# A diffusion layer's fill stage: second up column's weight sums made beside the mixing stage, last tiles' gated sums kept in accumulators, first token sums split ahead of the prompt's norm

## Chip, cores and metric

One core of a Trainium2 chip. Its engines run side by side, each in its own order: TensorE (PE) for matmuls, VectorE (DVE), ScalarE (ACT) and GpSimd (POOL) for elementwise work; SP's queue, and POOL's, issue DMA transfers. The metric is the device time of one execution in microseconds (us), the median of several runs. Profiles are of one execution each.

## What is computed

One layer over 1024 sample tokens and 128 prompt tokens of width 1024, all in 32-bit floats: a gated linear-attention mixer, then a convolutional feed-forward net, both with a residual. The edits lie where the one ends and the other begins:

```python
mix = merged @ w_out
x = x + gate1 * mix
h = rmsnorm(x, norm2) * (1 + scale2) + shift2
u = dw_conv(h @ w_up, conv_w, conv_b, grid)
gate, up = jnp.split(u, 2, axis=-1)
x = x + gate2 * ((silu(gate) * up) @ w_down)
```

FFN_HIDDEN is 2816, so `w_up` is 1024 x 5632. modulation (gate1, scale2, shift2) differs between sample and prompt.

## The kernel before

**Stages.** Up to about 730 us the mixer runs. Then the products with w_out for nine tiles of 128 tokens (0 to 7 sample, 8 prompt) with residual, norm and modulation, to about 790. Then 22 columns of 128 hidden units of the up-projection (L1724, L1925) with the convolution on DVE (L1862, L1879), to about 1284, and the products with w_down to the end.

**Splits.** Each 32-bit operand is a rounded high part (`hi`, made by ACT) and the rest (`lo`, by a subtraction in `split_lo`, L69), and a product is three matmuls: hi x hi, hi x lo, lo x hi.

**Up products.** A column's weights are 2 x 2 blocks ("11" to "22": row 1 the gate, row 2 the up half; 512 inputs each). With four sums of weights (s1 to s4) and four of token blocks (t1 to t4), seven products with names `up(c, 1)` to `up(c, 7)` replace eight block products. So each column needs eight weight blocks, hi and lo, and the tokens once need b11, b21, b22, t1, t2, t3 and t4, hi and lo. `half_hi` and `half_lo` split half a token block, `token_sum` makes a sum; `rb(i, j, n)` is a half of a raw token block, `tmp` are sums in the accumulator tiles `acc`. `up_prompt` are the same column's products with the prompt (tile `p`, parts ph and pl).

**Column 0's weights** are made beside the end of the mixer by `prepare_up()`: four loads into two tiles named up (one pair of blocks each), eight high parts (`up_hi`), eight low parts (four in tiles `up_lo`, four in place), four sums (L1294), and sixteen stores by POOL to scratch memory (scr_up, L1291). `up_hi` and `up_lo` come from the pool `fb`, which has two buffers (`fbp = pool(es1, "fb", 2)`). Their memory is used again by later pools of the w_out stage. SP later loads the parts from scratch into the weight slots W and W0 (`load_first`, L1746). **Later columns** get raw weights by `load_row`, sums by `weight_sums` (L1715 to L1718; column 1's on DVE, the rest on POOL), high parts by ACT (L1709) and low parts by POOL (`split_slots`, tiles wuh and wul).

**Tiles of tokens.** For a tile t: `head7(t)` or `heads(t, a, b)` are its products with w_out into an accumulator us[t] (pool of three in PSUM); `mult` (L1407) multiplies by the gate into xn, `add` (L1410) adds the residual xt and stores it, `square` (L1415, ACT) and `stat` (POOL's power, L1420) give the norm, `norm` (L1423, ACT) applies it. PE then transposes: `turn3(g, kt)` (L1431) for tiles 0 to 2 and 3 to 5 (groups 0 and 1), `turn2` (L1452) for 6 and 7, `turn_prompt` (L1468) for 8; `modulate3`, `modulate2` and `modulate_prompt` write the raw token blocks, half on DVE (L1364) and half on ACT (L1360). `load_mh(t)` and `load_xt(t)` are SP's loads of mixer output and residual for a tile.

**What sets the order.** Most instructions around the change go through `run(engine, ...)`, which ties each to the one before it on its engine, so engines run in the order in which the code is written; DMA issues follow their position and waits, and a buffer that is used again makes the next writer wait for the last reader. `ran["free"] = True` lifts the tie.

Of the kernel before, what the change touches and what calls it, by code (L numbers as in the profile page):

```python
# [13 lines left out]
ALU = mybir.AluOpType  # L14
# [35 lines left out]
def kernel(ctx: ExitStack, tc: tile.TileContext, ins, outs, stop=None):  # L50
# [46 lines left out]
    scr_up = [dram.tile([P, 8, 512], F32, name=f"scr_up{x}") for x in "hl"]  # L97
# [1173 lines left out]
    def prepare_up():  # L1271

        r = {}
        for row in (1, 2):
            t = rawp.tile([P, 2, 512], F32, name="up0", tag="raw")
            for half in range(2):
                nm = f"{row}{half + 1}"
                r[nm] = t[:, half]
                c0 = (row - 1) * HID
# [5 lines left out]
        def split(nm, place, keep):  # L1285
# [4 lines left out]
            for i, t in enumerate((hi, lo)):  # L1290
                nc.gpsimd.dma_start(scr_up[i][:, UP0.index(nm)], t.bitcast(F32))  # L1291
# [17 lines left out]
    prepare_up()  # L1309
# [37 lines left out]
    x4q = pool(es2, "x4", 1)  # L1347
    mhq = pool(es2, "mh", 1)
# [36 lines left out]
    us, xts, xns, sts, mhs_, turned = {}, {}, {}, {}, {}, {}  # L1385
# [18 lines left out]
    def mult(t):  # L1404
        q = {"n3": xaq, "n4": x4q}.get(X_OUT[t], xnq)
        xns[t] = q.tile([P, D], F32, name="xn2", tag=X_OUT[t])
        run("dve", lambda: tt(xns[t], us[t], gate1[0 if t == 8 else 1], op=ALU.mult))  # L1407

    def add(t):
        run("dve", lambda: tt(xts[t], xns[t], xts[t], op=ALU.add))  # L1410
        nc.gpsimd.dma_start(scr_x1[t], xts[t])

    def square(t):
        sts[t] = accs[0][:, 1024 + 2 * t : 1026 + 2 * t]
        run("act", lambda: nc.scalar.activation(xns[t], xts[t], AF.Square, accum_out=sts[t][:, 0:1]))  # L1415
# [6 lines left out]
    def norm(t):  # L1422
        run("act", lambda: nc.scalar.activation(xns[t], xts[t], AF.Copy, scale=sts[t][:, 1:2]))  # L1423
# [49 lines left out]
    def modulate_prompt(kt):  # L1473
        scaled(kt, 0, again["p"][:, kt, :], turned["p", kt // 4][:, kt % 4, :])
# [69 lines left out]
    for kt in range(0, KT, 2):  # L1544
# [26 lines left out]
    for kt in range(0, KT, 2):  # L1571
# [5 lines left out]
        if kt == 0:  # L1577
# [3 lines left out]
        if kt == 2:  # L1581
            stat(6)
            norm(6)
            load_xt(8)
    heads(7, 6, 8)
    token_sum(tmp[0], rb(0, 1, 0), rb(0, 0, 0))
    half_hi("b11", 1, rb(0, 0, 1))
    token_sum(tmp[2], rb(1, 1, 0), tmp[0])
    half_hi("b21", 1, rb(1, 0, 1))
    half_lo("b11", 1, rb(0, 0, 1))  # L1590
    half_lo("b21", 1, rb(1, 0, 1))
    mult(7)
    add(7)
    square(7)
    stat(7)
    norm(7)

    heads(8, 0, 5)
    wot = again["wo"]
    for nm in ("b22", "t2"):  # L1600
        for x in "hl":
            HB[x][nm] = wot.tile([P, 4, 512], F32R, name=f"{nm}{x}", tag="wo")
    half_hi("b22", 0, rb(1, 1, 0))
    half_lo("b22", 0, rb(1, 1, 0))
    turn2(0)
    turn2(1)
    heads(8, 5, 6)
    turn2(2)
# [666 lines left out]
```

## Time and profile before

| | us |
|---|---|
| median of 3 runs | 1565.24 (1563.28 to 1569.36) |
| profiled execution: its time | 1569.81 |
| profiled execution: its span | 1568.0 |
| PE busy | 1496.2 (95%) |
| DVE busy | 1148.0 (73%) |
| ACT busy | 782.1 (50%) |
| POOL busy | 706.0 (45%) |
| mean granted PE clock, of full | 0.985 |

The span runs from the first to the last instruction; the time also holds what lies around it, 1.8 us. Rows of a timeline begin with start and duration, and end with the idle time before them and what ended it. A window's row gives for each engine its busy time and, in brackets, its instructions, then PE's granted clock (1.00 is full), the share of the 16 DMA engines, and GB/s.

### The profile page before, as it was taken

What the parts mean: (1) busy time and instruction counts of PE and PEld (TensorE: products, weight loads), DVE (VectorE), ACT (ScalarE), POOL (GpSimd) and SP (SyncE); (2) the same over time, 40 slices, a digit from 0 to 9 for tenths busy, and PEclk for the clock granted to TensorE, in tenths of its full rate; (3) what the DMA queues carried; (4) which work ended last, traced back from release to release, by engine and by line L of the source; (5) the groups of instructions that cost most, each with busy time, mean ns of one, the idle gap of its engine ahead of it and who ended that gap; (6) DMA issues with size and microseconds to landing.
All of it is one profiled execution on the core that took longest, in us unless ns stands there. A gap on an engine that the chain in (4) does not pass through costs nothing.

```text
span 1568.0 us, 31139 instructions
## 1 busy us (share of the span) xinstructions
PE 1496.2 (95%) x12506; PEld 1260.1 (80%) x12506; DVE 1148.0 (73%) x1735; ACT 782.1 (50%) x1519; POOL 706.0 (45%) x538
## 2 busy tenths in 40 slices
PE   7999999999999989899888999999999998999997
PEld 2699989999898978677666888888888887788886
DVE  3657566565566667555569999999999999579565
ACT  3565567545454445513554444544444444457444
POOL 1512122334332240132126899999999996000001
PEclk9999999999999999999999999999999999999999
DMA  9311111336445452777541455455645566879763
GB/s 341 104 55 46 46 53 60 113 99 197 123 136 166 127 171 86 281 281 251 180 151 56 166 167 135 123 139 135 190 117 146 163 162 209 311 239 355 251 191 118
DMA packets 172939, 252.49 MB, mean 161 GB/s; under 512 B 11732, under 2 KB 113602, under 8 KB 170874
## 3 DMA queue, kind: packets, MB, share of 16 engines
q1 hardware_dynamic: 149591, 172.21, 34.4%
q0 software_dynamic: 22592, 77.60, 15.9%
q8 instruction: 98, 1.61, 0.4%
q10 hardware_dynamic: 611, 0.68, 0.1%
q14 instruction: 47, 0.39, 0.1%
HBM read 190.62 MB, written 82.90 MB: 174 GB/s over the span
## 4 chain that ended last, share of the span: by engine, by line
PE 72%; DVE 9%; DMA 6%; issue 4%; ACT 4%; POOL 3%; SPq 1%; POOLq 0%; ACTq 0%; DVEq 0%
PE u L1724 23%; PE mm L603 13%; PE xb L2137 6%; PE yb L2137 6%; PE mm L617 5%; PE x L1925 3%; DVE acc L1862 3%; PE mm L746 3%; PE lv L935 3%; PE yb L2188 2%; PE x L1003 1%; PE mm L506 1%; DMA raw<-in_w_in_dram 1%; DMA mh<-scr_m 1%; DMA wa<-in_w_ada_dram 1%
## 5 line engine op out<-in xcount | busy, mean ns | idle before, releaser
L1862 DVE SCALAR_TENSOR_TENSOR acc<-u,convc,acc 128x945 f32<-128x945 f32 (+2 forms) x352 | 426.8, 1218 | 8.4 <-ACT acc L1850 1.3
L69 POOL TENSOR_TENSOR wl<-raw,wh 128x1024 fp32r<-128x1024 f32 x42 | 103.5, 2467 | 241.4 <-ACT wh L132 182.7
L603 PE MATMUL mm<-h1h,wh 128*128 128x384 f32 x528 | 186.0, 352 | 1.1 <-ACT qj L515 1.1
L603 PE MATMUL mm<-h1l,wh 128*128 128x384 f32 x528 | 180.1, 341 | 0.0
L603 PE MATMUL mm<-h1h,wl 128*128 128x384 f32 x528 | 180.0, 341 | 0.0
L898 DVE TENSOR_TENSOR Q<-Q,fb 128x384 f32<-128x384 f32 x126 | 81.1, 644 | 90.9 <-PE lv L935 89.5
L69 POOL TENSOR_TENSOR wul<-sr,wuh 128x512 fp32r<-128x512 f32 (+1 forms) x65 | 118.2, 1819 | 28.2 <-ACT wuh L1709 28.0
L69 POOL TENSOR_TENSOR wul<-ra,wuh 128x1024 fp32r<-128x1024 f32 x44 | 111.6, 2536 | 20.0 <-ACT wuh L1709 17.5
L888 ACT ACTIVATE m<-k 128x384 f32<-128x384 f32 x126 | 70.3, 558 | 85.3 <-PE lv L935 40.1
L2112 POOL TENSOR_TENSOR sq<-sq,mhalf 128x1 f32<-128x1 f32 x9 | 11.0, 1229 | 215.5 <-DVE sq L2109 215.5
L603 PEld LDWEIGHTS mm<-h1h,wh 128*128 128x128 f32 x528 | 100.3, 190 | 6.0 <-issue 3.9
L603 PEld LDWEIGHTS mm<-h1l,wh 128*128 128x128 f32 x528 | 100.4, 190 | 0.6 <-issue 0.2
L603 PEld LDWEIGHTS mm<-h1h,wl 128*128 128x128 f32 x528 | 100.0, 189 | 0.8 <-issue 0.5
L617 PE MATMUL mm<-wh,h1h 128*128 128x256 f32 x288 | 83.7, 291 | 1.6 <-ACT v L642 1.5
L900 DVE TENSOR_TENSOR k<-k,fb 128x384 f32<-128x384 f32 x126 | 74.2, 589 | 13.1 <-ACT m L888 7.6
L617 PE MATMUL mm<-wh,h1l 128*128 128x256 f32 x288 | 80.4, 279 | 0.0
L617 PE MATMUL mm<-wl,h1h 128*128 128x256 f32 x288 | 80.3, 279 | 0.0
L132 ACT ACTIVATE wh<-raw 128x1024 fp32r<-128x1024 f32 x50 | 52.9, 1059 | 43.9 <-PE mm L603 11.3
L1709 ACT ACTIVATE wuh<-ra 128x1024 fp32r<-128x1024 f32 x42 | 44.3, 1055 | 45.5 <-issue 20.3
L1957 POOL TENSOR_TENSOR acc<-acc,acc 128x1152 f32<-128x1152 f32 x22 | 60.0, 2727 | 10.0 <-DVE acc L1862 10.0
L1890 ACT ACTIVATE u2p<-u 128x512 f32<-128x512 f32 x44 | 26.3, 598 | 71.3 <-PE u L1724 71.3
L1709 ACT ACTIVATE wuh<-sr 128x512 fp32r<-128x512 f32 (+1 forms) x63 | 48.7, 773 | 22.4 <-PE x L1925 17.0
(378 smaller groups left out, 4502.5 us busy)
## 6 DMA issues: line engine op xcount, KB each, us to landing
ra<-in_w_ffn_up_dram SPq DMA_DIRECT2D x84, 256.0 KB, 3.1
raw<-in_w_in_dram SPq DMA_DIRECT2D x32, 512.0 KB, 4.4
v<-in_w_ada_dram SPq DMA_DIRECT2D x27, 512.0 KB, 4.5
scr_g<-acc POOLq DMA_DIRECT2D x22, 576.0 KB, 5.5
scr_s<-late POOLq DMA_DIRECT2D x11, 1024.0 KB, 5.8
scr_t<-in_w_ffn_down_dram POOLq DMA_DIRECT2D x16, 704.0 KB, 7.2
wa<-in_w_ada_dram SPq DMA_DIRECT2D x16, 512.0 KB, 6.1
scr_t<-in_w_ffn_down_dram POOLq DMA_DIRECT2D x2, 2816.0 KB, 12.8
```

The costliest lines, as they stand in the source:

```text
L69: return eng.tensor_tensor(out, full, hi.bitcast(F32), op=ALU.subtract)
L132: nc.scalar.activation(hi, raw, AF.Copy)
L603: anchor["fill"] = mm(ps, a[:, kt, :], h[kt][b], start=(n == 0), stop=(n == 23))
L617: anchor["fill"] = mm(ps, h[kt][t // 3][:, ts_], a[:, kt % 4, :], start=(n == 0), stop=(n == 23))
L888: nc.scalar.activation(aps(t, 0, [[2 * h, NB], [h, 2], [1, h]]), aps(src, 0, [[2 * h, NB], [BL + h, 2], [1, h]]), AF.Copy)
L898: nc.vector.tensor_tensor(qm, qm, aps(ff_, 2 * h - 1, [[BL - h, 2], [2 * h, NB], [0, h]]), op=ALU.mult)
L900: nc.vector.tensor_tensor(km, km, aps(ff_, BL + 2 * h - 1, [[-(BL + h), 2], [2 * h, NB], [0, h]]), op=ALU.mult)
L1709: first = nc.scalar.activation(hi, raw, AF.Copy)
L1724: last = mm(dst, w_slot(c, a, x)[:, kt, :], HB[y][b][:, kt, :], start=(start and n == 0), stop=(stop and n == 11), skip_group_check=True,)
L1862: last = nc.vector.scalar_tensor_tensor(o, u3[:, r0 + dy : r1 + dy, c0 + dx : c1 + dx], wc(3 * (dy + 1) + dx + 1), o, op0=ALU.mult, op1=AL ...
L1957: last = nc.gpsimd.tensor_tensor(accg, accg, accu, op=ALU.mult)
L2137: anchor["down"] = mm(banks[i], w[a][:, ts_], w[b][:, 512:1024], start=(start and j == 0 and n == 0), stop=(j == NPAIR - 1 and n == 2), sk ...
```

## The change

1. `prepare_up(c)` runs for columns 0 and 1. `next_weights(1, ...)` then loads column 1's sixteen parts from scratch; column 1's `load_row`, its sums on DVE and its splits on ACT and POOL go. `load_row(2, ...)` is issued earlier.
2. For tiles above 4 the gate product stays in the accumulator: product, sum's input and square are there; `norm` alone takes a tile xn.
3. Tile 5's product, add and square move into group 0's loop; low parts and tile 6 to 8 steps are put in another order; the prompt's gate broadcast `gate_bc` (L1355) moves in among `heads(8, ...)`.
4. t1, half of b22 and the second token sum are made ahead of the prompt's norm (t1's tiles now lie where x4 and mh were); a token sum overwrites `rb(0, 0, 1)`. PE turns the prompt after `up(0, 5)` instead of before. `modulate_prompt` is all on ACT. The t4 sums and both sums into the accumulator F are made by `first_sums` ahead of `up(0, 7)`.

```diff
-    def prepare_up():
+    def prepare_up(c):
...
-                c0 = (row - 1) * HID
+                c0 = (row - 1) * HID + c * P
...
-                nc.gpsimd.dma_start(scr_up[i][:, UP0.index(nm)], t.bitcast(F32))
+                nc.gpsimd.dma_start(scr_up[c][i][:, UP0.index(nm)], t.bitcast(F32))
...
-    prepare_up()
+    for c in range(2):
+        prepare_up(c)
...
-    def mult(t):
+    def new_xn(t):
         q = {"n3": xaq, "n4": x4q}.get(X_OUT[t], xnq)
         xns[t] = q.tile([P, D], F32, name="xn2", tag=X_OUT[t])
-        run("dve", lambda: tt(xns[t], us[t], gate1[0 if t == 8 else 1], op=ALU.mult))
+        return xns[t]
+
+    def mult(t):
+        gated[t] = us[t] if t > 4 else new_xn(t)
+        run("dve", lambda: tt(gated[t], us[t], gate1[0 if t == 8 else 1], op=ALU.mult))
...
     def norm(t):
+        if t > 4:
+            new_xn(t)
...
     def modulate_prompt(kt):
-        scaled(kt, 0, again["p"][:, kt, :], turned["p", kt // 4][:, kt % 4, :])
+        run("act", lambda: nc.scalar.activation(
+            again["p"][:, kt, :], turned["p", kt // 4][:, kt % 4, :], AF.Identity, scale=s2[:, kt, 0:1], bias=b2[:, kt, 0:1]
+        ))
...
             norm(3)
+            mult(5)
         if kt == 2:
             square(4)
+            add(5)
         if kt == 4:
             stat(4)
             norm(4)
-    mult(5)
-    add(5)
-    square(5)
+            square(5)
     stat(5)
+    norm(5)
     half_hi("b11", 0, rb(0, 0, 0))
-    norm(5)
-    half_lo("b11", 0, rb(0, 0, 0))
     half_hi("b21", 0, rb(1, 0, 0))
-    half_lo("b21", 0, rb(1, 0, 0))
...
     half_hi("t2", 0, tmp[2])
-    half_lo("t2", 0, tmp[2])
+    token_sum(rb(0, 0, 1), rb(0, 1, 1), rb(0, 0, 1))
...
-    gate1[0] = again["late"].tile([P, D], F32, name="gate1_0", tag="gate")
-    gate_bc(gate1[0], (0, 1), 0)
-    ran["free"] = True
+    es2b.close()
+    es_t1 = ExitStack()
+    h2t1 = pool(es_t1, "h2t1", 1, side="right")
+    p1_t = h2t1.tile([P, 512], F32, name="cp1")
+    for x in "hl":
+        HB[x]["t1"] = h2t1.tile([P, 4, 512], F32R, name=f"t1{x}")
     mult(8)
     add(8)
+    half_hi("t1", 0, tmp[0])
+    half_hi("t1", 1, rb(0, 0, 1))
     square(8)
+    half_lo("t1", 0, tmp[0])
     stat(8)
+    half_lo("t1", 1, rb(0, 0, 1))
+    half_hi("b22", 1, rb(1, 1, 1))
     norm(8)
+    ran["free"] = True
     turn_prompt()
...
+    def next_weights(c, names):
+        if c == 1:
+            for nm in names:
+                load_first(c, nm)
+        else:
+            split_slots(c, names, nc.gpsimd)
...
-    load_row(1, 2)
-    load_row(1, 1)
...
+    load_row(2, 2)
+    load_row(2, 1)
...
-        run("dve", lambda: weight_sums(1, nc.vector))
+
+    def first_sums():
+
+        F = u[0][0]
+        new_tiles("t4", 1)
+        run("dve", lambda: tt(F[:, 0:512], F[:, 0:512], copies["p1"], op=ALU.add))
         for n in range(2):
             token_sum(tmp[2 + n], rb(1, 0, n), tmp[2 + n])
-        new_tiles("t4", 1)
+            half_hi("t4", n, tmp[2 + n])
+        run("dve", lambda: tt(F[:, 512:NS], F[:, 512:NS], copies["u2"], op=ALU.add))
         for n in range(2):
-            half_hi("t4", n, tmp[2 + n])
             half_lo("t4", n, tmp[2 + n])
```

SP's issues at the end of the mixer, of before (xt is a residual's tile, mh the mixer output of a tile, wl and wh parts of w_out; scr_pre_108 is tile 0's residual, scr_pre_109 tile 1's):

```order
L1395 DMA xt_9826<-scr_pre_108 128x1024
L1402 DMA mh<-scr_m_2_81 128x4x128
L1402 DMA mh<-scr_m_2_84 128x4x128
L1402 DMA mh<-scr_m_2_87 128x4x128
L1402 DMA mh<-scr_m_2_90 128x2x128
L1395 DMA xt_9828<-scr_pre_109 128x1024
L1402 DMA mh<-scr_m_2_81 128x4x128
L1402 DMA mh<-scr_m_2_84 128x4x128
L1402 DMA mh<-scr_m_2_87 128x4x128
L1402 DMA mh<-scr_m_2_90 128x2x128
L147 DMA wl<-scr_wo_98 128x1024
L147 DMA wh<-scr_wo_98 128x1024
```

and of the change, the same queue from the same point, where up are column 1's weights:

```order
L1280 DMA up_9751<-in_w_ffn_up_dram 128x4x128 x2
L1280 DMA up_9754<-in_w_ffn_up_dram 128x4x128 x2
L147 DMA wl<-scr_wo_98 128x1024
L147 DMA wh<-scr_wo_98 128x1024
L1346 DMA modrB<-scr_modB 128x512
L1397 DMA xt_9886<-scr_pre_110 128x1024
L1397 DMA xt_9888<-scr_pre_111 128x1024
L147 DMA wh<-scr_wo_91 128x1024
L147 DMA wl<-scr_wo_91 128x1024
L1397 DMA xt_9882<-scr_pre_108 128x1024
L1404 DMA mh<-scr_m_2_81 128x4x128
L1404 DMA mh<-scr_m_2_84 128x4x128
```

Column 1's loads stand where tile 0's residual stood, and that residual, the mixer output of tiles 6 and 7 (mh) and tile 1's residual stand behind the loads of w_out and of tiles 2 and 3.

DVE's instructions at the end of the mixer, of the change (up, up_hi and up_lo are column 1's; on, ev and mh the mixer's last; xn<-u is the gate product of tile 0). Before, none of the rows with up stood between the mixer's and the gate product:

```order
L1089 TENSOR_TENSOR on<-o,g 128x384
L752 TENSOR_TENSOR ev<-ev,v 128x512
L69 TENSOR_TENSOR up_9754<-up_9754,up_hi 128x512
L69 TENSOR_TENSOR mh_8781<-on,mh_8781 128x384
L69 TENSOR_TENSOR up_lo<-up_9751,up_hi 128x512
L1294 TENSOR_TENSOR up_9751<-up_9751 128x512
L69 TENSOR_TENSOR up_9751<-up_9751,up_hi 128x512 x2
L1413 TENSOR_TENSOR xn_9916<-u,gate_1_8783 128x1024
L1416 TENSOR_TENSOR xt_9882<-xn_9916,xt_9882 128x1024
```

Tile 0's gate product now stands behind column 1's last four low-part and sum instructions.

DVE's instructions in front of the first convolution (L1862 before, L1890 now), of before (L1715 to L1718 are column 1's weight sums):

```order
L1376 TENSOR_TENSOR acc_10288<-rb_9794,rb_9793 128x1024
L1364 TENSOR_SCALAR sr<-x,s_878,b_879 128x128 x4
L69 TENSOR_TENSOR pl<-sr,ph 128x1024
L2008 TENSOR_TENSOR u<-u,cp_10295 128x512
L69 TENSOR_TENSOR t3l<-acc_9784,t3h 128x4x256
L69 TENSOR_TENSOR t3l<-acc_10288,t3h 128x4x256
L1715 TENSOR_TENSOR sr<-ra 128x512
L1718 TENSOR_TENSOR sr<-ra 128x512
L1376 TENSOR_TENSOR acc_9785<-rb_9796,acc_9785 128x1024
L1376 TENSOR_TENSOR acc_10289<-rb_9796,acc_10289 128x1024
L2009 TENSOR_TENSOR u<-u,u2p_10293 128x512
L1716 TENSOR_TENSOR sr<-sr,ra 128x512
```

and of the change, from the same instruction:

```order
L1378 TENSOR_TENSOR acc_10355<-rb_9850,rb_9849 128x1024
L69 TENSOR_TENSOR pl<-sr,ph 128x1024
L69 TENSOR_TENSOR t3l<-acc_9840,t3h 128x4x256
L69 TENSOR_TENSOR t3l<-acc_10355,t3h 128x4x256
L1812 TENSOR_TENSOR u<-u,cp_10309 128x512
L1378 TENSOR_TENSOR acc_9841<-rb_9852,acc_9841 128x1024
L1378 TENSOR_TENSOR acc_10356<-rb_9852,acc_10356 128x1024
L1816 TENSOR_TENSOR u<-u,u2p_10360 128x512
L69 TENSOR_TENSOR t4l<-acc_9841,t4h 128x4x256
L69 TENSOR_TENSOR t4l<-acc_10356,t4h 128x4x256
L2053 TENSOR_TENSOR u<-u,u2p_10360 128x512
L1890 SCALAR_TENSOR_TENSOR acc_9840<-u,convc,acc_9840 128x15x63
```

The prompt's four modulations on DVE and column 1's four weight sums are gone from this stretch.

More of the change, by code (lines that the diff above doesn't have):

```diff
@@ L96 @@
     scr_s = [dram.tile([P, 4, 512], F32, name=f"scr_s{j}") for j in range(NPAIR)]
-    scr_up = [dram.tile([P, 8, 512], F32, name=f"scr_up{x}") for x in "hl"]
+    scr_up = [[dram.tile([P, 8, 512], F32, name=f"scr_up{c}{x}") for x in "hl"] for c in range(2)]
     scr_t = [dram.tile([NPAIR, P, 512], F32, name=f"scr_t{i}") for i in range(4)]
@@ L1602 @@
             HB[x][nm] = wot.tile([P, 4, 512], F32R, name=f"{nm}{x}", tag="wo")
+    gate1[0] = again["late"].tile([P, D], F32, name="gate1_0", tag="gate")
+    gate_bc(gate1[0], (0, 1), 0)
     half_hi("b22", 0, rb(1, 1, 0))
     half_lo("b22", 0, rb(1, 1, 0))
+    heads(8, 4, 5)
     turn2(0)
     turn2(1)
-    heads(8, 5, 6)
-    turn2(2)
-    turn2(3)
-    heads(8, 6, 8)
+    heads(8, 5, 7)
     modulate2(0)
```

101 lines of the change are left out of this document (53 added, 48 removed).

## The prediction

> **What bounds the kernel now.** I read the page first, then the table of time windows, then the waits of TensorE (PE) in the stretch that the edits touch.
>
> ```profile
> span 1568.0 us, 31139 instructions
> PE 72%; DVE 9%; DMA 6%; issue 4%; ACT 4%; POOL 3%; SPq 1%; POOLq 0%; ACTq 0%; DVEq 0%
> core 0: us, PE busy (x) PEld busy (x) DVE busy (x) ACT busy (x) POOL busy (x), PEclk, DMA share, GB/s
> 720.00:730.00 10.00, 8.86 (x50) 7.17 (x48) 5.05 (x10) 3.71 (x15) 1.78 (x2) 1.00 0.48 146
> 760.00:770.00 10.00, 7.47 (x33) 5.52 (x32) 6.09 (x10) 4.61 (x9) 1.14 (x2) 0.83 0.31 105
> 800.00:810.00 10.00, 9.05 (x28) 7.05 (x28) 7.10 (x9) 4.25 (x8) 2.39 (x1) 0.66 0.33 129
> 820.00:830.00 10.00, 5.31 (x20) 3.50 (x19) 10.00 (x11) 5.26 (x7) 6.46 (x4) 0.88 0.36 103
> 900.00:1280.00 380.00, 379.67 (x1861) 314.62 (x1860) 368.87 (x389) 176.71 (x237) 365.98 (x245) 1.00 0.54 147
> ```
>
> The chain that ended last lies on PE for 72%. The last window is the steady state of the up columns: PE is full, and nothing in it is edited, so the change moves the time only by when that state begins. The edits lie between 700 and 870 us. There PE is not full, and its granted clock falls to 0.66 of full in one window: an idle spell is paid for once as idleness and again as slow matmuls behind it. What PE waits for there:
>
> ```profile
> PE u L1724 <- DVE t4l L69: 3.0, 1, 3.0
> PE x L1431 <- ACT xn L1423: 2.8, 2, 1.7
> PE u L1724 <- DVE acc L1862: 2.4, 2, 1.6
> PE x L1468 <- ACT xn L1423: 2.0, 1, 2.0
> PE x L1431 <- DVE rb L1364: 1.9, 2, 1.3
> PE u L1724 <- DVE t3l L69: 1.2, 1, 1.2
> ```
>
> Columns are total, times, longest. No wait exceeds 3 us, and most end with VectorE (DVE). DVE is 10.00 of 10 busy at 820 to 830: in front of the first convolution it is the engine that ends last. So there are two accounts: DVE is relieved behind the w_out products, and a chain of stores is added in front of them.
>
> **The front: column 1's sums added (a loss).** prepare_up(1) adds 4 loads on SP, 8 high splits on ACT, 8 low splits and 4 sums on DVE and 16 stores on POOL. Their busy time is small: 8 x 0.63 us on ACT, 12 x 0.69 on DVE, 16 x 0.54 on POOL. The price is their chain. The high parts and four of the low parts share the pool "fb" of two buffers, so a new part waits until an older one's store has landed:
>
> ```profile
> L1288 ACT ACTIVATE up_hi<-up x8: 625/632/632, 666.8 to 703.6; 128x512 fp32r<-128x512 f32 x8
> L69 DVE TENSOR_TENSOR up<-up,up_hi x4: 684/691/693, 686.0 to 704.2; 128x512 fp32r<-128x512 f32 x4
>   ACT up_hi L1288: 14.0, 2
> DMA to landing us min/median/max: 2.3/4.8/8.5
> 705.49 0.54 POOL L1291 DMA_DIRECT2D scr_upl<-up  x1
> 714.62 0.21 ACT L1047 ACTIVATION_READ_ACCUMULATOR on<-o 128x1 f32 x1
> scr_uph<-up_hi POOLq DMA_DIRECT2D x2, 256.0 KB, 7.9
> ...
> scr_uph<-up_hi POOLq DMA_DIRECT2D x2, 256.0 KB, 3.0
> ```
>
> The third row says that ACT waited 14.0 us in two waits for these stores in column 0 alone. The last two rows are median landings: 7.9 us for stores issued at 684 to 692, 3.0 at 700 to 710. Column 1's second pair of weights loads into a buffer that column 0's last store (issued 705.49) frees, at about 708.8; landed, the first high part finds ACT free at about 714.9, behind the row at 714.62. Twelve tiles through two buffers make six rounds with five landings between them. A round is 0.63 (ACT) + 0.54 (POOL) + 0.2 + the landing L, so L + 1.4. I take L = 3.0, the row nearest in time, because DMA is only 0.48 busy at 720 to 730. The front's sixth round begins at 714.9 + 5 x 4.4 = 736.9, and two high parts and a low part later, 2.5 us, DVE is through at 739.4. The bounds are 2.3 (5 x 0.7 = 3.5 us earlier) and 4.8 (9 us later).
>
> The Trainium skill (DMA: Bandwidth & Descriptors, "Anatomy of one DMA — SWDGE (gpsimd) path") puts a GpSimd store at about 2.0 us plus bytes over 436 GB/s; that would be 2.6 us for 256 KB, an estimate from the page, and the sum 2 us better. The median of 4.8 here disagrees, so it sets nothing.
>
> What queues behind it:
>
> ```profile
> 707.99 2.62 SPq L1402 DMA_DIRECT2D mh<-scr_m  x4
> mh<-scr_m SPq DMA_DIRECT2D x6, 256.0 KB, 5.6
> xt<-scr_pre SPq DMA_DIRECT2D x5, 512.0 KB, 5.2
> 731.78 1.22 DVE L1407 TENSOR_TENSOR xn<-u,gate 128x1024 f32<-128x1024 f32 x1 [0.82 <-PE u L1484]
> 736.74 1.22 DVE L1410 TENSOR_TENSOR xt<-xn,xt 128x1024 f32<-128x1024 f32 x1
> 737.87 1.22 DVE L1407 TENSOR_TENSOR xn<-u,gate 128x1024 f32<-128x1024 f32 x1
> 739.14 0.73 PE L1503 MATMUL u<-wh,mh 128*128 128x512 f32 x2 [0.53 <-DVE xn L1407]
> ```
>
> The gate product of tile 0 (731.78) now stands behind that last low part in DVE's order: 739.4. On SP's queue tile 6's four loads (707.99, 2.62 us for four issues) now stand behind the whole chain, because they write memory that the last buffers of "fb" hold: about 741.8. Tile 1's residual now stands behind these four and two more, so it is issued at 741.8 + 6 x 0.65, near 745.7, and lands some 5 us later, near 750.7. DVE's add of tile 1 (736.74) waits for it, and the gate product of tile 3 (737.87) behind it frees the accumulator for which PE waits at 739.14. PE so goes on near 752.8: 13.5 us late. It has no other work from 738.6 on, so it comes back cold. The window at 800 to 810, after idle spells of 1 to 2 us, ran at 0.66, 3.4 us lost; I take 2 us more here. **Front: +15.5 us**, 11 at L = 2.3, 24 at L = 4.8.
>
> The Trainium skill (TensorE: Matmul & The Clock Gate, "Part 1: The HAM clock gate") says that one idle window of about 3.4 us drops the clock to half, and a busy one restores it. By it the 14 us idle would be paid with one window at half rate, 1.7 us of PE's work lost, an estimate from that page. It speaks against the change; the trace agrees in kind, and its 3.4 us are more than one window's.
>
> **The middle: tiles 5 to 8 (a gain).** Gate product, add and square of tile 5 move into group 0's loop and the norm goes ahead of the high parts, so the transposes of group 1 need not wait:
>
> ```profile
> 759.02 0.66 PE L1431 MATMUL x<-ident,xn 128*128 128x128 f32 x4 [1.68 <-ACT xn L1423]
> ```
>
> That is 1.7 us, and 1.9 us are the two waits for DVE's rb (the low parts in front of it move later). The window at 760 to 770 was at 0.83, 1.7 us lost, which goes with the wait. **-5.3 us**; if the late loads of the front starve this group, nothing. That the gate product of tiles above 4 stays in the accumulator saves no instruction: the same product, add and square read PSUM, as the product did before at 1.22 us. I price it at zero; a tenth of 1.22 us on each of the twelve would be +1.5.
>
> **The back: from the end of the w_out products to the first convolution (a gain).**
>
> ```profile
> 788.40 1.98 PE L1355 MATMUL x<-modrB,ident 128*128 128x512 f32 x4
> 797.81 1.09 PE L1468 MATMUL x<-ident,xn 128*128 128x128 f32 x8 [1.96 <-ACT xn L1423]
> 828.28 1.19 DVE L1862 SCALAR_TENSOR_TENSOR acc<-u,convc,acc 128x945 f32<-128x945 f32 x1
> 815.59 2.88 DVE L1715 TENSOR_TENSOR sr<-ra 128x512 f32<-128x512 f32 x1
> L69 DVE TENSOR_TENSOR t4l<-acc,t4h 128x1024 fp32r<-128x1024 f32 x2 | 3.2, 1590 | 0.0
> L69 DVE TENSOR_TENSOR t1l<-acc,t1h 128x1024 fp32r<-128x1024 f32 x2 | 2.4, 1222 | 2.8 <-ACT t1h L1379 2.8
> 835.67 0.35 DVE L1879 SCALAR_TENSOR_TENSOR acc<-x,convc,acc 128x127 f32<-128x127 f32 x1 [2.14 <-ACT acc L1875]
> 795.46 0.39 PE L1724 MATMUL u<-b21h,w 128*128 128x512 f32 x1
> ```
>
> Before, 39.9 us pass from 788.40 to 828.28. DVE spends 5.4 of them on column 1's weight sums (2.88, and 0.68, 1.19 and 0.68 from their own rows of the same view); these instructions go, with ACT's high and POOL's low splits of column 1. With POOL's splits goes what happens beside them: t4l takes 1590 ns against 1222 for t1l of the same shape, and the first sum 2.88 us against 0.68 of its sibling. The t1 splits and sums no longer wait for the prompt's norm (2.8 us in t1l's row, 1.96 on PE), and four modulations of the prompt pass to ACT.
>
> After, counted on DVE from the end H of the products: 1.0 for the last rb, then ten instructions of 128x1024 (gate product and add of tile 8, t1l twice, a token sum, t2l twice, b22l, two t3 sums) at 1.14 apart: H + 12.4. The prompt's low part pl cannot start there, because PE turns the prompt only after up(0,5): 24 matmuls to 795.46, 5.7 us from their start, 12 more at the same pace 2.8, the turn 1.1, so H + 9.7 or so; ACT's eight modulations and one copy take 3.8, and pl ends at H + 14.7. Behind it stand t3l twice, two t4 sums and t4l twice (6.8) and three halves of 0.6: H + 23.3, and 1.4 for small waits. The convolution so starts at H + 24.7, **15.2 us** earlier. I take 14, since column 1's s1 parts, which SP now loads from scratch behind the first half of the prompt's product, land when PE has just come to them (rivals). The bounds are 10 and 17.
>
> The stall of 2.14 at 835.67 is ACT's, which waited for a product of a PE at half clock. PE now stands ahead of the convolution, so I take **-2**. The gate broadcast of the prompt (1.98 at 788.40) moves in among tile 8's products, where it fills a wait: zero, and +1.4 if it fills none.
>
> **Sum.** +15.5 - 5.3 - 14 - 2 = -5.8 us. The profiled run took 1569.81 us, 4.57 above the median of the three runs, 1565.24, so the sum is taken from the median: **1559 us**. With all bounds of the forecast's own case (front 12 to 19, back 12 to 16) it reads 1554 to 1565.
>
> **The rivals.**
> 1. *The store chain is longer (slower).* Place: the five landings in "fb". Price: 5 us for each us of L. The sum is zero at L = 4.2, and at the 5.2 to 6.5 of a stretch like 684 to 692 (7.9) it is +5 to +12: 1570 to 1577, and it decides for slower from L = 5.8. For it: the median of 4.8, and SP's loads of wl, wh and two residuals in that stretch. Against it: tiles 6 and 7 are loaded only behind it, which leaves DMA emptier than before.
> 2. *The chain is shorter or partly hidden (faster).* At 2.3 the front costs 11 to 12, and the back gives 16: 1553 (11.5 - 5.3 - 16 - 2 = -11.8). For it: the last stores of column 0 landed in about 3.0. Against it: PE has nothing else to do meanwhile.
> 3. *The back gives half.* Column 1's sixteen parts come from scratch through SP, four at a time behind a slot that PE frees; if each lands in the 5.6 of the other 256 KB loads rather than in 3, PE waits 2 to 3 us at two or three places and DVE's head start is lost: back 8 instead of 14, time 1565. For it: these loads are issued close to their use. Against it: DVE, not PE, ends that stretch.
>
> **Chances.** Forecast 0.45, first rival 0.25 (some of it inside no change), second 0.2, third 0.1. A measurement of this kernel can tell about 0.5% from no change, 7.8 us: faster is below 1557.4, slower above 1573.1. The forecast's case holds a little under half of its chance below 1557.4 (its sum is -11 to 0): 0.2; with the second rival that is 0.4. Slower is the upper part of the first, 0.18. The rest, 0.42, is no change. The range from 1549 to 1575 takes in the second rival's and most of the first's; the forecast's own is 1554 to 1565.
>
> **What would show it.** In the changed profile the waits of ACT's up_hi for scr_up stores should grow by about 10 us, PE's first product of tile 6 should start near 752 with an idle time before it of over 10 us, and the clock should drop there. From the end of tile 8's products to the first convolution some 25 us should pass, with no wait of PE for t4l, and PE should be as full as now in the steady columns. If tile 6's products start before 745 the front is wrong; if more than 30 us pass in the back, the account of DVE is.

## The result, and the profile after

| | before | after |
|---|---|---|
| median of 20 runs each, us | 1564.53 (1558.69 to 1569.36) | 1568.9 (1563.86 to 1573.02) |
| ratio | 1 | 1.0027, interval 1.0016 to 1.0039 |
| profiled execution: its time, us | 1569.81 | 1563.86 |
| its span, us | 1568.0 | 1562.1 |
| PE busy | 1496.2 (95%) | 1486.5 (95%) |
| mean granted PE clock | 0.985 | 0.983 |

The change costs 0.27%, some 4.3 us. That is more than the interval allows for chance and less than the 0.5% that the prediction calls a change. The two profiled executions say the opposite of the medians: the one of after is the shortest of its 20 runs, the one of before is longer than any of its 20. So absolute times of the two profiles are not compared below. I count from a place that both kernels share and reach in unchanged code, the first ScalarE (ACT) activation `on<-o` of 128x128 elements behind 690 us (713.95 before, 707.45 after; "start" from here on), to five marks: the gate product of tile 0 on VectorE (DVE), TensorE's (PE) first product of tile 6, its first up product, the first convolution on DVE, the first w_down product.

| us from start | tile 0's gate product | tile 6 | first up product | first convolution | first w_down product | end of span |
|---|---|---|---|---|---|---|
| before | 17.83 | 25.19 | 75.87 | 114.33 | 597.11 | 854.05 |
| after | 30.71 | 48.59 | 93.28 | 119.01 | 598.38 | 854.65 |

Tile 6 comes 23.4 us late, 18.7 of these are won back by the first convolution, 3.4 more by w_down, and 1.3 us of loss are left there. Two executions of the kernel before differ by 0.6 us at that last mark and by 1.6 at the end (e8 below), so the 1.3 is near the spread.

Windows of after. A window's columns are as in the prediction: PE, its weight loads, DVE, ACT, GpSimd (POOL), granted clock, DMA share, GB/s.

```profile
720.00:730.00 10.00, 7.12 (x32) 5.38 (x30) 4.97 (x9) 3.49 (x8) 4.35 (x8) 1.00 1.00 354
730.00:740.00 10.00, 0.57 (x1) 0.50 (x2) 4.49 (x6) 1.26 (x2) 1.17 (x3) 0.57 0.80 285
740.00:750.00 10.00, 6.47 (x18) 4.67 (x16) 3.06 (x4) 2.29 (x3) 2.71 (x5) 0.67 0.87 252
750.00:760.00 10.00, 3.96 (x9) 3.14 (x10) 4.80 (x5) 3.25 (x5) 2.60 (x3) 0.50 0.76 263
820.00:830.00 10.00, 4.08 (x20) 3.38 (x19) 9.41 (x8) 3.37 (x4) 6.98 (x4) 0.68 1.03 376
900.00:1280.00 380.00, 380.00 (x1862) 314.96 (x1861) 369.16 (x391) 177.04 (x237) 366.45 (x245) 1.00 0.53 146
```

The last row is the steady state, as full as before. The second to fourth are new: PE works 0.57 of 10 us at 730 to 740, and the clock stays between 0.50 and 0.67 until 760. DMA is 1.00 busy at 720 to 730. These ten microseconds lie 12.55 us behind start; the ten that lie as far behind it in before are 726.5 to 736.5, and there DMA is 1.00 busy too. PE's waits from 724 to 866 of after (total, times, longest):

```profile
PE u L1494 <- DVE xn L1413: 10.1, 1, 10.1
PE u L1513 <- DVE xn L1413: 9.6, 1, 9.6
PE u L1743 <- DMA wuh<-scr_up1h: 5.9, 1, 5.9
PE u L1494 <- DMA wh<-scr_wo: 2.2, 1, 2.2
PE u L1743 <- ACT u2p L1918: 0.3, 1, 0.3
```

Where no wait was longer than 3 us, two of about 10 stand now, both for gate products, and one of 5.9 for column 1's parts from scratch. The waits that the change was priced to remove (for t4l, t3l, rb, xn) are gone.

**The chain of stores**, in ACT's timeline of after. The second and third round began at 712.45 and 716.49; these are the starts of the first, the fourth (with its second part), the fifth and the sixth:

```profile
708.21 0.64 ACT L1288 ACTIVATE up_hi<-up 128x512 fp32r<-128x512 f32 x1
...
720.47 0.63 ACT L1288 ACTIVATE up_hi<-up 128x512 fp32r<-128x512 f32 x1 [2.58 <-DVE on L1089]
726.08 0.63 ACT L1288 ACTIVATE up_hi<-up 128x512 fp32r<-128x512 f32 x1 [3.80 <-DMA scr_up1l<-up_lo]
728.62 0.63 ACT L1288 ACTIVATE up_hi<-up 128x512 fp32r<-128x512 f32 x1 [1.50 <-DMA scr_up1h<-up_hi]
735.85 0.63 ACT L1288 ACTIVATE up_hi<-up 128x512 fp32r<-128x512 f32 x1 [6.59 <-DMA scr_up1h<-up_hi]
```

Three rounds take 12.3 us, 4.1 each, where 4.4 was priced (the second round begins without an idle time on ACT, behind the mixer's steps, so most of its landing is hidden). The last two take 15.4 us, 7.7 each. The parts at 726.08, 728.62 and 735.85 wait for stores that POOL issued 7.1, 7.2 and 6.3 us before:

```profile
718.94 0.54 POOL L1291 DMA_DIRECT2D scr_up1l<-up_lo  x1 [0.98 <-DVE up_lo L69]
...
721.40 0.54 POOL L1291 DMA_DIRECT2D scr_up1h<-up_hi  x1 [0.18 <-issue]
...
729.55 0.54 POOL L1291 DMA_DIRECT2D scr_up1h<-up_hi  x1 [0.94 <-ACT up_hi L1288]
```

What runs beside them is in SyncE's (SP) queue of after and in a second table of windows:

```profile
717.80 0.34 SPq L147 DMA_DIRECT2D wl<-scr_wo  x1
719.21 5.70 SPq L1397 DMA_DIRECT2D xt<-scr_pre  x2
724.96 0.48 SPq L147 DMA_DIRECT2D wh<-scr_wo  x1
725.54 0.40 SPq L147 DMA_DIRECT2D wl<-scr_wo  x1
```

```profile
714.00:720.00 6.00, 5.58 (x35) 4.72 (x34) 4.32 (x10) 2.67 (x11) 2.51 (x5) 1.00 0.50 165
720.00:726.00 6.00, 3.80 (x19) 2.96 (x18) 3.81 (x7) 1.81 (x5) 2.30 (x4) 1.00 0.95 318
726.00:735.80 9.80, 3.31 (x15) 2.42 (x13) 2.55 (x4) 1.68 (x3) 2.68 (x5) 0.78 0.94 364
```

Six loads of 512 KB and one of 256 KB leave SP between 717.8 and 725.9: four parts of w_out, the residuals of tiles 2 and 3, and a piece of the modulation. Up to 720 DMA is half busy and the rounds are short; from 720 on it is 0.95 busy and they are long.

This full stretch is not the change's work. In before the same loads, with one residual less, leave SP from 723.91 to 727.58, beginning 10 us behind start as here, and before's own rows show what that does to a store of this size from POOL's queue (the windows, then the stores issued at 719 to 735):

```profile
714.00:724.00 10.00, 9.97 (x61) 8.58 (x60) 3.65 (x9) 4.89 (x25) 2.75 (x3) 1.00 0.52 162
724.00:732.00 8.00, 6.76 (x33) 5.41 (x32) 4.53 (x10) 1.82 (x5) 2.32 (x3) 1.00 0.85 285
scr_pre<-ev POOLq DMA_DIRECT2D x2, 256.0 KB, 6.6
```

Cut at 725, DMA in before is 0.05 busy from 720 and 0.97 busy from 725 to 736. The same two stretches, measured from start, are 0.05 to 0.06 and 0.95 to 0.99 busy in e1, e5, e8 and e9 below, none of which has column 1's stores there, and the same two stores take 6.4 to 6.5 us. Which of the loads makes the stores slow was not tried apart.

Behind the chain, in the timelines of POOL, SP, DVE and PE:

```profile
740.40 0.55 POOL L1291 DMA_DIRECT2D scr_up1h<-up_hi  x1 [3.09 <-issue]
```

```profile
742.93 4.55 SPq L1404 DMA_DIRECT2D mh<-scr_m  x6
747.60 0.55 SPq L1397 DMA_DIRECT2D xt<-scr_pre  x1
```

```profile
738.16 1.22 DVE L1413 TENSOR_TENSOR xn<-u,gate 128x1024 f32<-128x1024 f32 x1
753.63 1.23 DVE L1416 TENSOR_TENSOR xt<-xn,xt 128x1024 f32<-128x1024 f32 x1 [10.44 <-DMA xt<-scr_pre]
```

```profile
756.04 1.22 PE L1513 MATMUL u<-wh,mh 128*128 128x512 f32 x2 [9.57 <-DVE xn L1413]
```

POOL issues the last high part's store 3.09 us after it could have; tile 6's mixer output (mh) waits for that store, tile 1's residual (xt) for the six issues in front of it, DVE's add for the residual, and PE's tile 6 for the gate product behind that add.

### The profile page after: what moved, and what is told of

Same layout as the page of the kernel before. It is cut to its first block, busy times and chain, and to the rows that moved or that the text cites. A ratio compares the mean times of both kernels' runs of the same rounds, so it can differ in the third digit from the quotient of the medians.

```text
span 1562.1 us, 31203 instructions
## 1 busy us (share of the span) xinstructions
PE 1486.5 (95%) x12506; PEld 1255.9 (80%) x12506; DVE 1148.2 (74%) x1739; ACT 783.7 (50%) x1526; POOL 708.4 (45%) x549
## 4 chain that ended last, share of the span: by engine, by line
PE 79%; DMA 6%; DVE 5%; issue 3%; ACT 3%; POOL 3%; SPq 0%; POOLq 0%; ACTq 0%; DVEq 0%
PE u L1743 27%; PE mm L603 13%; PE mm L617 6%; PE xb L2170 6%; PE yb L2170 6%; PE x L1954 4%; PE mm L746 3%; PE lv L935 3%; PE u L1513 2%; PE yb L2221 2%; DVE acc L1890 1%; PE x L1003 1%; PE mm L506 1%; DMA raw<-in_w_in_dram 1%; DMA mh<-scr_m 1%
## 5 line engine op out<-in xcount | busy, mean ns | idle before, releaser
L1890 DVE SCALAR_TENSOR_TENSOR acc<-u,convc,acc 128x945 f32<-128x945 f32 (+2 forms) x352 | 426.7, 1217 | 9.7 <-ACT acc L1878 2.7
L898 DVE TENSOR_TENSOR Q<-Q,fb 128x384 f32<-128x384 f32 x126 | 85.2, 676 | 90.5 <-PE lv L935 88.8
L69 POOL TENSOR_TENSOR wul<-sr,wuh 128x512 fp32r<-128x512 f32 (+1 forms) x62 | 111.8, 1804 | 20.8 <-ACT wuh L1728 20.6
L69 POOL TENSOR_TENSOR wul<-ra,wuh 128x1024 fp32r<-128x1024 f32 x42 | 107.1, 2550 | 11.8 <-ACT wuh L1728 8.8
L1984 ACT ACTIVATE acc<-acc 128x1152 f32<-128x1152 f32 x22 | 25.7, 1170 | 66.5 <-DVE acc L1890 66.5
## 6 DMA issues: line engine op xcount, KB each, us to landing
scr_t<-in_w_ffn_down_dram POOLq DMA_DIRECT2D x2, 2816.0 KB, 12.9
```

Source lines behind the costliest of these rows:

```text
L69: return eng.tensor_tensor(out, full, hi.bitcast(F32), op=ALU.subtract)
L898: nc.vector.tensor_tensor(qm, qm, aps(ff_, 2 * h - 1, [[BL - h, 2], [2 * h, NB], [0, h]]), op=ALU.mult)
L1890: last = nc.vector.scalar_tensor_tensor(o, u3[:, r0 + dy : r1 + dy, c0 + dx : c1 + dx], wc(3 * (dy + 1) + dx + 1), o, op0=ALU.mult, op1=AL ...
```

## Experiments

Every run is timed against runs of the kernel before on the same chip. The marks from start repeat to about 0.1 us up to the convolution where the code in front of them is the same, so they carry the attributions, and the ratios the verdicts. All ratios lie within 2% of one, and all intervals but e6's exclude one.

| us from start | gate product | tile 6 | first up | convolution | w_down | end | ratio to before, interval |
|---|---|---|---|---|---|---|---|
| e1_no_col1 | 17.83 | 25.19 | 68.30 | 99.55 | 577.25 | 835.25 | 0.9896, 0.9872 to 0.9919 |
| e2_col1_only | 31.09 | 49.19 | 100.56 | 133.54 | 614.05 | 870.45 | 1.0116, 1.0094 to 1.0139 |
| e3_four_buffers | 21.47 | 40.60 | 84.71 | 111.52 | 591.34 | 847.54 | 0.9973, 0.9959 to 0.9988 |
| e4_residuals_first | 30.61 | 40.48 | 93.14 | 119.94 | 598.41 | 854.74 | 1.0034, 1.0018 to 1.005 |
| e5_sums_on_pool | 17.83 | 25.19 | 68.33 | 98.84 | 576.97 | 832.77 | 0.986, 0.9837 to 0.9883 |
| e6_four_buffers_residuals | 20.25 | 35.61 | 88.63 | 115.43 | 593.91 | 850.17 | 0.9993, 0.9981 to 1.0005 |
| e7_row2_later | 30.82 | 48.66 | 93.24 | 118.78 | 597.88 | 854.09 | 1.0032, 1.002 to 1.0044 |
| e8_before_again | 17.82 | 25.17 | 75.86 | 114.34 | 597.75 | 852.41 | one run, 1570.58 us |
| e9_t1_late | 17.73 | 25.08 | 68.22 | 103.97 | 582.11 | 839.39 | 0.9935, 0.9912 to 0.9959 |

### Part 1 undone, and part 1 alone

e1 is the kernel after with column 1's sums made as before:

```diff
-    for c in range(2):
-        prepare_up(c)
+    prepare_up(0)
...
-        if c == 1:
-            for nm in names:
-                load_first(c, nm)
-        else:
-            split_slots(c, names, nc.gpsimd)
+        split_slots(c, names, nc.gpsimd)
...
+    load_row(1, 2)
+    load_row(1, 1)
...
-    load_row(2, 2)
-    load_row(2, 1)
...
+        run("dve", lambda: weight_sums(1, nc.vector))
```

> Part 1 undone alone: column 1's weights are loaded raw, summed on DVE (behind the t3 splits) and split by ACT and POOL in column 0, as before; parts 2 to 4 stay. Theory A (the front chain is the whole loss, parts 3 and 4 are gains): no front cost, heads(6) starts as in before; the middle keeps -3 to -5 us; from tile 8's products to the first convolution 31 to 34 us instead of 39.9 before and 25.6 with the change; about -10 us against before (ratio 0.992 to 0.995). Rival B (the gain in the back hangs on part 1, since DVE is full there): within 3 us of before.

e2 is the kernel before with these lines the other way round, and nothing else of the change.

> Part 1 alone on the kernel before. Theory A: PE's first product of tile 6 comes 20 to 25 us later than in before, the back gives 7 to 9 us (5.4 of sums, 1.8 of what POOL's splits cost beside them), so +12 to +17 us (ratio 1.008 to 1.011). Rival B (the chain is mostly hidden or the back gives all it gives through part 1): within 3 us of the whole change, +2 to +6 us.

Parts 2 to 4 alone make the kernel 1.04% faster (some 16 us), part 1 alone makes it 1.16% slower (some 18 us). The difference of the two is the whole within their intervals. In e1 the front is to the hundredth of a microsecond that of before (17.83, 25.19): all 23.4 us of the delay are part 1's. Both are larger than expected (0.992 to 0.995 and 1.008 to 1.011). What part 1 gives behind the front is small: from the first up product to the convolution after needs 25.73 us and e1 31.25, so 5.5 us. By e2 against before it is the same 5.5 (32.98 against 38.46). The 7 to 9 us that were expected of it there did not come. PE's waits of e2 have the two long ones of after; those for xn and rb, which parts 2 to 4 were to remove, stay as in before, the one for t4l is gone, and the one for t3l grows from 1.2 to 3.0:

```profile
PE u L1504 <- DVE xn L1408: 10.7, 1, 10.7
PE u L1485 <- DVE xn L1408: 10.6, 1, 10.6
PE u L1725 <- DVE t3l L69: 3.0, 1, 3.0
PE x L1469 <- ACT xn L1424: 2.0, 1, 2.0
PE x L1432 <- DVE rb L1365: 1.9, 2, 1.3
```

### Four buffers for the chain of stores

e3 is the kernel after whose high parts and kept low parts come in turn from "fb" and from "k", another pool of two buffers of the same size that stands unused then:

```diff
+    up_turn = []
+
+    def part(name):
+        up_turn.append(name)
+        q, tag = ((fbp, "fb"), (kp, "k"))[len(up_turn) % 2]
+        return q.tile([P, 512], F32R, name=name, tag=tag)
...
-            hi = fbp.tile([P, 512], F32R, name="up_hi", tag="fb")
-            lo = fbp.tile([P, 512], F32R, name="up_lo", tag="fb") if keep else r[place].bitcast(F32R)
+            hi = part("up_hi")
+            lo = part("up_lo") if keep else r[place].bitcast(F32R)
```

> The change with four buffers for the high and low parts (the pool fb and the two buffers of k, idle by then, in turn). Theory A (a round of the chain is a landing, two buffers make six rounds): the gate product of tile 0 comes 6 to 9 us earlier than with the change, PE's first product of tile 6 as well, and the time is 6 to 9 us under the change (ratio to before 0.997 to 0.999). Rival C (the stores are held by the DMA traffic of that stretch, not by the number of buffers): the same last store, within 2 us of the change.

The gate product comes 9.2 us earlier than in after and tile 6 8.0 us; the ratio falls from 1.0027 to 0.9973, 8.4 us, which puts it below one. So the landings between the rounds are what delayed the gate product. What is left of the front, 3.6 us there and 15.4 at tile 6, is SP's order, in DVE's timeline of e3:

```profile
732.93 1.23 DVE L1420 TENSOR_TENSOR xn<-u,gate 128x1024 f32<-128x1024 f32 x1 [1.62 <-PE u L1501]
741.05 1.23 DVE L1423 TENSOR_TENSOR xt<-xn,xt 128x1024 f32<-128x1024 f32 x1 [6.90 <-DMA xt<-scr_pre]
749.65 1.23 DVE L1423 TENSOR_TENSOR xt<-xn,xt 128x1024 f32<-128x1024 f32 x1 [4.82 <-DMA xt<-scr_pre]
```

The product no longer waits for column 1 but for PE; the residuals of tiles 0 and 1 now end DVE's idle times, since they still stand behind loads of w_out and of tiles 2 and 3 in SP's queue.

### The residuals of tiles 0 and 1 first

e4 is the kernel after in which tiles 0 and 1, not 2 and 3, take the pools "xa" and "xb" that are free early:

```diff
-    X_IN = {2: "xa", 3: "xb", 6: "xa", 7: "xb", 8: "xa"}
+    X_IN = {0: "xa", 1: "xb", 6: "xa", 7: "xb", 8: "xa"}
```

> The change, with the residuals of tiles 0 and 1 in the buffers xa and xb and those of 2 and 3 in the pool that column 1's raw weights use. Theory A (half of the front is the residual of tile 1, which waits behind column 1's last store and six loads of mixer output): DVE's add of tile 1 waits no more, PE's first product of tile 6 comes when its mixer output has landed, 6 to 9 us earlier than with the change; time 5 to 8 us under it (ratio to before 0.998 to 1.000). Rival D (residuals 2 and 3 then take the same place in the chain): DVE waits as long for tile 2, time within 2 us of the change.

Theory A's first half holds and its time does not: tile 6 starts 8.1 us earlier and the first up product at the same time as in after (93.14, 93.28), with a ratio no better (1.0034 against 1.0027). DVE's adds of the next tiles wait instead:

```profile
764.82 1.23 DVE L1416 TENSOR_TENSOR xt<-xn,xt 128x1024 f32<-128x1024 f32 x1 [5.67 <-DMA xt<-scr_pre]
769.93 1.23 DVE L1416 TENSOR_TENSOR xt<-xn,xt 128x1024 f32<-128x1024 f32 x1 [3.89 <-DMA xt<-scr_pre]
```

So the time at which PE's tile 6 begins is not by itself what the front costs: what is won there is lost again where later residuals come, as rival D said. e6 has both edits, e3's and e4's.

> The change with both the four buffers and the residuals of tiles 0 and 1 in xa and xb. Theory A (the front is two waits one behind the other, the chain and what is loaded behind it): the gate product of tile 0 at 21 to 22 us from the mixer's last ACT step at which the markers begin, PE's first product of tile 6 at 31 to 35 instead of 48.6 with the change, tile 8's end some 10 to 13 us earlier; time 1553 to 1558, still above the run without column 1 (1548). Rival D (what is won at tile 6 is lost at the residuals of tiles 2 to 5, as with residuals alone): tile 8's end as with four buffers alone (84.7), time within 2 us of 1559.

Its tile 6 is 5.0 us ahead of e3's and its first up product 3.9 behind; the ratio is 0.9993 against 0.9973, with intervals that overlap, and the 1553 to 1558 us of theory A are missed (median 1563.07). PE's waits of e6 show where it went:

```profile
PE u L1520 <- DMA mh<-scr_m: 7.8, 1, 7.8
PE x L1446 <- DVE acc L1432: 6.1, 2, 3.5
```

Tile 6's own input and the statistics of later tiles wait now. In these two runs the order that brings tiles 0 and 1 first only passes the delay on.

### Column 2's weights later

After waits 5.9 us on PE for column 1's parts from scratch. e7 is the kernel after that loads column 2's raw weights where the kernel before loads a next column's, to take them out of the way:

```diff
-    load_row(2, 2)
-    load_row(2, 1)
...
-            if 2 < n + 1 < NHID:
+            if n + 1 < NHID:
...
-            if 2 < n + 1 < NHID:
+            if n + 1 < NHID:
```

> The change, with the raw weights of column 2 loaded at their place in column 0's loop, behind the first parts of column 1, not ahead of them. PE waited 5.9 us for column 1's s1 part. Theory A (DVE ends last in the back, so that wait lies beside DVE's work): the wait falls to 1 to 3 us, the first convolution starts as before this edit, time within 2 us of the change. Rival F (the wait is on the path): time 3 to 5 us under the change.

The wait is still 5.3 us, where theory A had 1 to 3, and a window of e7 shows DMA as full as in after:

```profile
PE u L1743 <- DMA wuh<-scr_up1h: 5.3, 1, 5.3
```

```profile
820.00:830.00 10.00, 6.38 (x40) 5.47 (x38) 9.48 (x8) 4.35 (x6) 4.09 (x3) 1.00 1.11 351
```

Raw weights are not what holds these parts up; the parts themselves are the likely traffic, which wasn't tried apart. The convolution (118.78 against 119.01) and the ratio hardly move. Since the wait hardly moved either, the run does not test whether it is on the path; the traces do, below.

### Sums on POOL, and t1 late

e5 is e1 with one edit: column 1's four weight sums, 5.7 us of DVE's time in front of e1's convolution (0.68, 2.89, 0.68 and 1.43), are made by POOL.

```diff
-        run("dve", lambda: weight_sums(1, nc.vector))
+        weight_sums(1, nc.gpsimd)
```

> As the run without column 1 in the fill stage (0.9896 of before), with column 1's four weight sums on POOL instead of DVE, at the same place. Theory A (in the back DVE ends last, and its 4.9 us of sums are all that part 1 still had to give there): from tile 8's products to the first convolution 26 to 28 us instead of 31.3, 3 to 5 us off the time, ratio to before 0.986 to 0.988. Rival E (POOL's sums come late for the splits of s1 to s4, or hold DVE's instructions beside them): PE waits for a low part of column 1 instead, time within 2 us of that run or above it.

The convolution moves by 0.7 us. DVE's and POOL's timelines of e5:

```profile
796.49 3.43 DVE L69 TENSOR_TENSOR t3l<-acc,t3h 128x1024 fp32r<-128x1024 f32 x2
805.51 4.43 DVE L69 TENSOR_TENSOR t4l<-acc,t4h 128x1024 fp32r<-128x1024 f32 x2 [0.52 <-ACT t4h L1380]
```

```profile
806.62 2.25 POOL L1733 TENSOR_TENSOR sr<-ra 128x512 f32<-128x512 f32 x1
808.83 2.25 POOL L69 TENSOR_TENSOR wul<-sr,wuh 128x512 fp32r<-128x512 f32 x1
811.16 1.30 POOL L1736 TENSOR_TENSOR sr<-ra 128x512 f32<-128x512 f32 x1
```

In e1 both pairs of DVE took 2.35 us. Here POOL runs beside them and they take 3.43 and 4.43, while POOL's own 128x512 take 2.25 instead of the 1.30 of the last row, which no such DVE pair overlaps. What POOL takes off DVE it takes back in lengthened instructions, as rival E had it: 30.5 us pass from the first up product to the convolution, not the 26 to 28 of theory A. e5 has the lowest time of all kernels run (0.986, the ratio that theory A named), ahead of before and of after; against e1 (0.9896) the intervals overlap, so a gain from this edit is not shown.

e9 is e1 with the splits of t1, and one of b22, put back behind the prompt's norm:

```diff
-    half_hi("t1", 0, tmp[0])
-    half_hi("t1", 1, rb(0, 0, 1))
...
-    half_lo("t1", 0, tmp[0])
...
-    half_lo("t1", 1, rb(0, 0, 1))
-    half_hi("b22", 1, rb(1, 1, 1))
...
         half_hi("t2", 1, tmp[3])
+        half_hi("t1", 0, tmp[0])
+        half_hi("t1", 1, rb(0, 0, 1))
+        half_lo("t1", 0, tmp[0])
+        half_lo("t1", 1, rb(0, 0, 1))
+        half_hi("b22", 1, rb(1, 1, 1))
```

> The kernel with part 1 undone (e1), with the five half splits of t1 and b22 put back behind the prompt's norm, as they stood before. In e1 31.25 us pass from the first up product to the first convolution, against 38.46 in the kernel before, and the gain of 7.2 has not been divided between part 4's two moves: t1 made early, and the prompt turned behind up(0,5) with the t4 sums late. Theory A: t1 made early is part of it. DVE then has its two low halves (1.2 us each before) and the wait of 2.8 us that stood in t1l's row behind the norm again, so the convolution comes 3 to 5 us later against the mixer's end, at 102.5 to 104.5, and PE waits for t1 again; time ratio to the kernel before 0.992 to 0.993. Rival B: DVE fills the norm's wait with other work whichever way, and only the order of the later sums counts: the convolution stays within 1 us of 99.55, and the ratio at 0.9896.

Everything up to the first up product is as in e1; the convolution comes 4.4 us later, at 103.97, and the ratio is 0.9935. DVE's row of the first low half of t1, and PE's waits of e9:

```profile
789.01 1.23 DVE L69 TENSOR_TENSOR t1l<-acc,t1h 128x1024 fp32r<-128x1024 f32 x1 [3.53 <-DMA wuh<-scr_up0h]
```

```profile
PE u L1737 <- ACT t1h L1380: 1.7, 1, 1.7
PE u L1737 <- DVE t1l L69: 0.9, 1, 0.9
```

Theory A holds: an idle time of 3.53 us is back on DVE, the engine that ends this stretch. The row names a load as what ended it, but the high part t1h that it reads is made by ACT until 788.98, and PE's waits name t1h too. So of the 7.2 us that parts 2 to 4 win between the first up product and the convolution (38.46 before, 31.25 in e1), 4.5 are t1 (with a half of b22) made early and 2.7 the rest.

### The kernel before, once more

> The kernel before, profiled once more, for the spread of the markers between two executions of one kernel. If the stretch from the mixer's last step to the first product with w_down is again near 597 us, the profile of before was typical; if it is near 593, some 3 to 4 us of what the two profiles differ by is spread.

Its marks up to the convolution are those of the first profile to 0.02 us; w_down differs by 0.6 and the end by 1.6, and its start is at 716.39 and not at 713.95. Over all profiles the start lies between 707.45 (after) and 716.86 (e4, the same code up to there). So the marks up to the convolution can be trusted to tenths, those behind it to 1 or 2 us, and absolute times of single profiles only to some 5 us.

Part 2 could not be taken out alone, since the gate product of tile 5 stands in an order that needs its accumulator; it wasn't tried.

## Why the prediction was wrong, and where it was right

The forecast was 1559 us, faster; the kernel became slightly slower, 1568.9. That is inside the wide range of 1549 to 1575 and outside the 1554 to 1565 of the forecast's own case.

**What bounds the kernel: right.** The steady columns are full in both (379.67 and 380.00 of 380), so the change counts by when they begin.

**The front: the mechanism right, the size wrong; the landing time L of the five rounds is the step that failed.** The prediction said: "I take L = 3.0, the row nearest in time, because DMA is only 0.48 busy at 720 to 730." That 0.48 is the mean of a nearly idle and a full half (0.05, then 0.97 from 725 on), and the row of 3.0 is of stores issued at 700 to 710, ahead of both. By the prediction's own count the fourth and fifth rounds begin at 728.1 and 732.5, in the full half, where the stores of 256 KB that POOL issued took 6.6 us in before. With 3.0 for three landings and 6.6 for two, an estimate from these rows, five rounds are 3 x 4.4 + 2 x 8.0 = 29.2 us. By ACT's rows they took 735.85 - 708.21 = 27.6 us, not 22.0; by the same count a landing was 27.6 / 5 - 1.4 = 4.1 on the mean: 2.7 in the first three rounds, 6.3 in the last two. So at the gate product the delay is 12.9 us where 7.6 was counted, and e3, which takes the landings away, gives 9.2 back at that mark. An estimate of 2.6 us for such a store, from the fit of the Trainium skill (DMA: Bandwidth & Descriptors, "Anatomy of one DMA — SWDGE (gpsimd) path"), is near the 2.3 to 3.0 us of the stores issued up to 717.42 and far from the 6.2 to 7.6 of those from 718.94 to 729.55; the prediction set it aside for a 3.0 that erred the same way.

From the gate product on, the prediction had 13.4 us to tile 6 (739.4 to 752.8), and 17.9 passed. Step by step: to mh's issue 4.8 instead of 2.4 (POOL's store came 3.09 us late), to the residual's 4.7 instead of 3.9, its landing 6.0 instead of 5.0, to PE 2.4 instead of 2.1. Front and tail together are +23.4 where 13.5 stood; with what the cold clock is taken to cost (from tile 6 to the first up product 44.69 us in after, 43.11 in e1: 1.6, where 2 stood) the term is **+25.0 instead of +15.5**, just above its own upper bound of 24. (By its count the bounds come to 12 and 24.5; it wrote 11 and 24.)

**The middle: right, a little small.** In e1, without the cold start, tile 6 to the first up product takes 43.11 us, before 50.68: -7.6. The prediction's -5.3, with the prompt's gate broadcast (1.4 by its count, taken to cost nothing at its new place) is -6.7 between these marks. The waits for xn and rb on which it rests are gone in after and stay in e2; which edit of parts 2 and 3 removes them was not tried apart.

**The back: right.** From the end of tile 8's products to the first convolution 39.9 us became 25.7 (119.01 - 93.28), where 24.7 was counted: -14.2, and -14 was taken. DVE ends it: from the low part pl (813.90) to the convolution (826.46) it idles for 0.5 us. PE's wait of 5.9 us for the parts from scratch, the third rival's mechanism, is there but lies beside DVE, as argued against that rival: it runs from 821.7 to 827.6, behind column 0's last product and past the convolution's start. What the prediction did not see is that only 5.5 of the 14 are part 1's: parts 2 to 4 alone bring 7.2 between these marks without a front (e1).

**The stall: right in kind.** Convolution to w_down takes 479.4 us, before 482.8: -3.4, where -2 was taken. The idle time of 2.14 us that DVE had there is gone:

```profile
833.89 0.34 DVE L1907 SCALAR_TENSOR_TENSOR acc<-x,convc,acc 128x127 f32<-128x127 f32 x1
```

What the rest is stays open; 0.6 us can be the spread of the last mark.

**The sum.** Between the marks, with the prediction's terms sorted to them:

| us | predicted | measured |
|---|---|---|
| up to tile 6 | +13.5 | +23.4 |
| tile 6 to the first up product: middle, gate broadcast, cold clock | -4.7 | -6.0 |
| first up product to convolution | -12.6 | -12.7 |
| convolution to w_down | -2.0 | -3.4 |
| sum | -5.8 | +1.3 |

The front missed by 9.9 and the others gave 2.8 back. The timed difference is +4.3, 2.5 to 6.1 by its interval. What lies between it and the +1.3 is in front of the start or behind w_down, where single profiles differ by as much; it was not located.

**The rivals.** The first rival's arithmetic was better than its chance: it put the zero of the sum at L = 4.2, and at the measured 4.1 the result is near zero. That it comes so near is partly luck: at 4.1 its arithmetic has a front of 21, which measured 25, and the other terms gave 2.8 more than priced. For it stood SP's loads of wl, wh and two residuals in that stretch, which is what the rows show; against it, that tiles 6 and 7 loaded late would leave DMA emptier, and it was as full as before. The signs named for the front came: ACT's waits for column 1's stores are 8.9 and 4.2 us,

```profile
ACT up_hi L1288 <- DMA scr_up1h<-up_hi: 8.9, 3, 6.6
ACT up_hi L1288 <- DMA scr_up1l<-up_lo: 4.2, 2, 3.8
```

where about 10 were named, tile 6 starts behind an idle time of 9.57 us with another of 10.1 ahead of it, where one of over 10 was named, and the clock falls to 0.50. Tile 6 starts at 756.04, not near 752, and measured from start it is later still.

## What to carry to other kernels

The landing time of a store that a change adds is read where its chain will run: in windows short enough to part an idle half from a full one, and from stores of the same size and queue in that very stretch. Here a mean of 0.48 hid 0.05 and 0.97, and the kernel before already had stores of 6.6 us in the full half. When a chain of stores goes through a pool of two buffers, every landing that no other work hides is paid; two more buffers were worth 8 us here for nothing else. And price each part of a change apart: parts 2 to 4 were worth 16 us, and part 1, which gave 5.5 us where it was meant to help, cost 25 ahead of it.

## What the hardware showed that was not expected

**DVE and POOL lengthen each other.** Beside each other, a pair of 128x1024 subtractions on DVE went from 2.35 to 4.43 us and a 128x512 on POOL from 1.30 to 2.25. The lengthening of each, about 1 us an instruction, is near what the other's instruction takes alone. The Trainium skill (SBUF — State Buffer, "Who interferes with whom") says that a VectorE instruction with two inputs in SBUF contends with a GpSimd instruction that reads SBUF, and that contention for the ports they share is an exclusive lock; these rows agree with it. Moving 5.7 us of work from the one to the other brought the convolution only 0.7 us forward in e5.

**A store issue on POOL stood still.** The row at 740.40 begins 3.09 us behind the one in front of it and waits for nothing that the profile shows, while its part was written at 737.5. The same store of e2 and e4 begins 3.68 and 3.34 us late in the same way. DVE works at 738 to 743 in after; whether that holds it up wasn't tried.
